# Staging the diagonal blocks of the gated delta rule with ScalarE copies instead of a masked product and a strided sum

## The chip, the cores and the metric

The kernel runs on one core of a Trainium2 chip. The core has five engines, each with its own instruction stream that it works off in order: TensorE (PE; its weight loads are shown as PEld), VectorE (DVE), ScalarE (ACT), GpSimd (POOL) and SyncE (SP), which here only issues DMA transfers. The metric is the device time of one execution in microseconds (us); of several executions the median is given.

## The reference, cut to what matters

The kernel computes a two-layer decoder trunk for one sequence of 512 positions and width 1024. The first layer mixes the sequence with a gated delta rule (8 heads of 128), the second with differential attention; each is followed by an MLP of width 4096. The change lies in the gated delta rule:

```python
kb = kc * bc[..., None]
a_mat = jnp.where(strict, jnp.einsum('bhnik,bhnjk->bhnij', kb, kc) * decay, 0.0)
rhs = jnp.concatenate([vc * bc[..., None], kb * jnp.exp(gcum)[..., None]], axis=-1)
sol = lax.linalg.triangular_solve(eye + a_mat, rhs, left_side=True, lower=True, unit_diagonal=True)
```

For every head and every chunk of the sequence a unit lower triangular matrix (identity plus `a_mat`) has to be inverted, or a system with it solved. The reference uses chunks of 64 positions; the kernel uses four chunks of 128, which gives the same result, and works with the transposed matrix.

## The kernel before, in words

The kernel goes through its stages in the order of the reference: norm and modulation, the projections of the first layer with the gated delta rule inside them, the output projection, the first MLP, attention, the second MLP. Weights come in with SyncE's DMAs (`weights`, L288 to L297): ScalarE rounds a block to a high part (L293), VectorE or GpSimd takes the low part (L284), and PE multiplies three times (`three`, L299 to L302). Beside that, VectorE works off 112 dot products for the conditioning vector, a few at each weight block (`mod_dot`, L193).

The function `gdn(h)` (from L509) does one head of the delta rule and is a generator with three parts. Its first part builds the matrices and inverts them, the second runs over the four chunks in sequence, the third normalises the output. The loop at L730 projects head after head and starts each head's first two parts, then finishes the head before.

Within the first part the steps that matter here are these.

1. L549 to L559: for each of the four chunks PE forms two 128x128 products in a PSUM bank "a" (tag "pa"; there are two such banks), and VectorE scales them into the SBUF tile "bq" (L558). A half of "bq" holds two chunks, each as the matrix B (128 columns) followed by the matrix ATT (128 columns). B is the transposed triangular matrix; `B(n)` and `ATT(n)` pick them for chunk n.
2. L568 to L574: the eight 16x16 blocks on each B's diagonal are taken out. VectorE multiplies B by a mask that is one in these blocks (`m_sub`, tile "db"), and sums over the eight block columns, so that row p keeps 16 values, those of its own block (tile "dc": 128 partitions x 4 chunks x 16).
3. L575 to L578: "dc" is written to a tile "d1" in DRAM and read back as "mt", with one 16x16 block on each of 32 partitions (4 chunks x 8 blocks). Both are DMAs of SyncE's queue; the read waits until the write has landed.
4. L579 to L587: 15 steps of a triangular solve on "mt", two VectorE instructions each (L584, L586), invert the 32 blocks.
5. L588 to L595: the inverses go through DRAM once more ("d2", back as "tc") and are spread to the diagonals of 128x128 tiles "t" (L593).
6. L596 to L639: PE, VectorE and ScalarE join blocks of 16 to blocks of 32, 64 and 128 ("t", "z", "um", "pi"), with copies on ScalarE at L624.
7. L641 to L654: this head's v and q are transposed by PE (L513, banks "pa") and read out by ScalarE (L649 and L520).

The second part (from L657) uses "z" and "ATT". All tiles named here but "d1", "d2" (DRAM) and the PSUM banks lie in one SBUF pool, `g_pool`, where tiles of one tag take turns in `bufs` buffers.

Nothing in the source fixes the order in which an engine meets work of different heads. The tile framework plans each engine's order when the program is built, by the order in the source as priority and by its own estimate of when operands are ready; it also places the semaphores. On the chip each engine then follows its fixed order.

Of the kernel before, what the change touches and what calls it, by code (L numbers as in the profile page):

```python
# [10 lines left out]
F32 = mybir.dt.float32  # L11
F32R = mybir.dt.float32r
AF = mybir.ActivationFunctionType
ALU = mybir.AluOpType
AX = mybir.AxisListType
PSUM = bass.MemoryType.PSUM

P = 128
D = 1024
KT = D // P  # L20
S = 512
# [8 lines left out]
SUB = 16  # L30
# [55 lines left out]
def trunk_kernel(ctx: ExitStack, tc: tile.TileContext, a, outT):  # L86
    nc = tc.nc
    V, G, A, T = nc.vector, nc.gpsimd, nc.scalar, nc.tensor
# [3 lines left out]
    def nm(s):  # L92
        count[0] += 1
        return f"{s}_{count[0]}"

    def open_pool(name, side="left", bufs=1):
        st = ExitStack()
        p = st.enter_context(tc.tile_pool(name=nm(name), bufs=bufs, side=side, reuse_waits="tile"))
        return p, st
# [14 lines left out]
    dp = ctx.enter_context(tc.tile_pool(name="dp", bufs=3, space=bass.MemoryType.DRAM))  # L114
# [13 lines left out]
    def big(pool, tag, bufs, dt=F32):  # L128
        return pool.tile([P, S], dt, tag=tag, name=nm(tag), bufs=bufs)
# [10 lines left out]
    def v3(ap, n=P):  # L140
        return ap.rearrange("p (u f) -> p u f", f=n)
# [231 lines left out]
    for k in range(KT):  # L373
        n = NE[k]
# [53 lines left out]
    g_pool, g_st = open_pool("g", "right")  # L428
# [10 lines left out]
    def gt_(name):  # L439
        return cp.tile([P, NT, H], F32, name=name)  # L440

    u, e, w, l, g = gt_("g_u"), gt_("g_e"), gt_("g_w"), gt_("g_l"), gt_("g_g")
# [58 lines left out]
    def uu(t, n):  # L501
        return t[:, n * P:(n + 1) * P]

    def m4(ap):
        return ap.unsqueeze(1).to_broadcast([P, 4, P])

    m_sub = mask[:, M_L1:M_L1 + P]

    def gdn(h):  # L509
# [36 lines left out]
        V.tensor_tensor(out=sj, in0=sj, in1=beta[:, :, h], op=ALU.mult)  # L546


        bq = [big(g_pool, "bq", 6) for _ in range(2)]  # L549
        for n in range(2):  # L550
            ps = bank("a")
            for c in (2 * n, 2 * n + 1):
# [3 lines left out]
            for c in (2 * n, 2 * n + 1):  # L556
                o = (c % 2) * 256
                V.scalar_tensor_tensor(out=v3(bq[n][:, o:o + 256]), in0=v3(ps[:, o:o + 256]), scalar=sj[:, c:c + 1],  # L558
                                       in1=uu(ex, c).unsqueeze(1).to_broadcast([P, 2, P]), op0=ALU.mult, op1=ALU.mult)  # L559
# [5 lines left out]
            return bq[n // 2][:, (n % 2) * 256 + P:(n % 2) * 256 + 256]  # L565


        db = big(g_pool, "db", 1)  # L568
        for n in range(2):
            V.tensor_tensor(out=v3(db[:, n * 256:(n + 1) * 256]),  # L570
                            in0=bq[n].rearrange("p (u t f) -> p u t f", u=2, t=2)[:, :, 0, :],
                            in1=m_sub.unsqueeze(1).to_broadcast([P, 2, P]), op=ALU.mult)
        dc = g_pool.tile([P, 4, SUB], F32, tag="dc", name=nm("dc"), bufs=2)
        V.tensor_reduce(out=dc, in_=db.rearrange("p (u b c) -> p u c b", u=4, c=SUB), axis=AX.X, op=ALU.add)  # L574
        d1 = dp.tile([4, P, SUB], F32, tag="d1", name=nm("d1"))  # L575
        nc.sync.dma_start(d1.rearrange("u p c -> p u c"), dc)
        mt = g_pool.tile([32, SUB, SUB], F32, tag="mt", name=nm("mt"), bufs=2)
        nc.sync.dma_start(mt.rearrange("p r c -> p (r c)"), d1.rearrange("u (b r) c -> (u b) (r c)", r=SUB))  # L578
        xv = g_pool.tile([32, SUB, SUB], F32, tag="xv", name=nm("xv"), bufs=2)  # L579
        pr = g_pool.tile([32, SUB, SUB], F32, tag="pr", name=nm("pr"), bufs=2)  # L580
        G.tensor_copy(xv, eye)
        for s in range(SUB - 1):
            shp = [32, SUB - 1 - s, s + 1]
            V.tensor_tensor(out=pr[:, s + 1:, :s + 1], in0=mt[:, s, s + 1:].unsqueeze(2).to_broadcast(shp),  # L584
                            in1=xv[:, s, :s + 1].unsqueeze(1).to_broadcast(shp), op=ALU.mult)
            V.tensor_tensor(out=xv[:, s + 1:, :s + 1], in0=xv[:, s + 1:, :s + 1], in1=pr[:, s + 1:, :s + 1],  # L586
                            op=ALU.subtract)  # L587
# [6 lines left out]
                        in0=tc_.unsqueeze(2).to_broadcast([P, 4, P // SUB, SUB]),  # L594
                        in1=m4(m_sub).rearrange("p u (b c) -> p u b c", c=SUB), op=ALU.mult)  # L595
# [20 lines left out]
        for b in (32, 64):  # L616
# [13 lines left out]
            if b == 32:  # L630
                p0, p1 = parts[0]
                for n in range(4):
# [3 lines left out]
                                in1=v3(pz[p1, 0:4 * b], b), op=ALU.subtract)  # L636
            for p0, p1 in parts:
                V.tensor_tensor(out=v3(z)[p0, :, p1], in0=v3(z)[p0, :, p1], in1=v3(pz[p0, 0:4 * b], b),
                                op=ALU.subtract)  # L639
# [28 lines left out]
        for c in range(NT):  # L668
            r = uu(vn, 0)
            if c > 0:  # L670
# [5 lines left out]
                r = g_pool.tile([P, P], F32, tag="r", name=nm("r"), bufs=2)  # L676
# [53 lines left out]
    for h in range(H):  # L730
        proj_head(h)
        heads.append(gdn(h))
        next(heads[h])
        next(heads[h])
        if h:
            next(heads[h - 1], None)
# [275 lines left out]
```

## Time and profile before

| what | us |
|---|---|
| median of 3 runs | 1369.26 |
| lowest and highest of them | 1368.76, 1371.17 |
| profiled execution | 1367.7 |
| its span, first to last instruction | 1365.9 |
| PE busy | 1304.3 |
| DVE busy | 829.7 |
| ACT busy | 558.8 |
| POOL busy | 471.1 |

Busy times are of the profiled execution and are unions: two overlapping instructions of one engine count once. Consecutive matmuls overlap, so that PE can be busy without a gap and still not be at its highest rate. In rows of groups the columns are line, engine, operation, tiles written and read, shapes and count, then total busy time, mean duration of one in ns, and the engine's idle time just before them with what ended it. In rows of a timeline the first two numbers are start and duration in us, counted from the start of the span. In rows of waits the columns are total, number and longest.

### The profile page before, as it was taken

Reading aid. Unit: us, or ns where it says so; the run is one execution under the profiler, and the core shown is the slowest. Engines: PE = TensorE matmul, PEld = TensorE weight load, DVE = VectorE, ACT = ScalarE, POOL = GpSimd, SP = SyncE. Lnnn points to the kernel's source line nnn. Section 1 sums busy time; section 2 is a strip of 40 time slices with the busy share of each in tenths; the row PEclk is TensorE's granted clock in tenths of the full one; section 3 lists DMA queues with packets and bytes.
Section 4 is the critical chain, followed back from the end, with each engine's and each line's share of the span. In section 5 each row is a group of like instructions: output and inputs, shape, how many; then the busy total and the mean of one; then the engine's idle time right before and its main releaser. Section 6 shows DMA issues by size and latency. Waiting matters only on the chain. (4 is left out here: it accounts for less than half of the span.)

```text
span 1365.9 us, 19395 instructions
## 1 busy us (share of the span) xinstructions
PE 1304.3 (95%) x7240; PEld 1097.0 (80%) x7240; DVE 829.7 (61%) x1632; ACT 558.8 (41%) x1175; POOL 471.1 (34%) x281
## 2 busy tenths in 40 slices
PE   4888999999999999999999999999999999999997
PEld 4666878777799888888888978888898888888886
DVE  6979899787847887778851777777453200031113
ACT  3396556553535342234422453444344421143221
POOL 4324132220015444444443021232144444444441
PEclk9999999899999999999999999999999999999998
DMA  9633323125624767766642232222123322232221
GB/s 316 213 93 96 107 71 93 37 75 141 209 103 146 252 222 243 242 229 228 221 154 93 66 120 86 66 67 66 62 79 110 105 94 93 100 102 93 93 77 62
DMA packets 113214, 174.98 MB, mean 128 GB/s; under 512 B 16384, under 2 KB 56992, under 8 KB 113120
## 3 DMA queue, kind: packets, MB, share of 16 engines
q1 hardware_dynamic: 112416, 172.92, 39.7%
q8 instruction: 57, 0.93, 0.3%
q10 hardware_dynamic: 704, 0.83, 0.2%
q14 instruction: 37, 0.30, 0.1%
HBM read 170.04 MB, written 2.62 MB: 126 GB/s over the span
## 5 line engine op out<-in xcount | busy, mean ns | idle before, releaser
L284 POOL TENSOR_TENSOR wl<-raw,wh 128x1024 fp32r<-128x1024 f32 (+1 forms) x137 | 330.1, 2410 | 392.1 <-ACT wh L293 392.1
L293 ACT ACTIVATE wh<-raw 128x1024 fp32r<-128x1024 f32 (+2 forms) x217 | 216.2, 997 | 468.6 <-PE pj L301 242.9
L300 PE MATMUL pj<-h,wh 128*128 128x512 f32 (+1 forms) x816 | 291.2, 360 | 12.4 <-ACT h L278 6.7
L302 PE MATMUL pj<-h,wl 128*128 128x512 f32 (+1 forms) x816 | 290.5, 358 | 1.9 <-DVE wl L284 1.9
L301 PE MATMUL pj<-h,wh 128*128 128x512 f32 (+1 forms) x816 | 291.2, 357 | 0.0
L193 DVE SCALAR_TENSOR_TENSOR mw<-mw,one,cs 128x1024 f32<-128x1024 f32 x96 | 209.4, 2194 | 47.5 <-ACT one L213 47.3
L300 PEld LDWEIGHTS pj<-h,wh 128*128 128x128 f32 x816 | 155.7, 191 | 33.3 <-ACT h L278 8.8
L302 PEld LDWEIGHTS pj<-h,wl 128*128 128x128 f32 x816 | 156.2, 192 | 20.1 <-DVE wl L284 2.6
L301 PEld LDWEIGHTS pj<-h,wh 128*128 128x128 f32 x816 | 156.4, 192 | 17.1
L302 PE MATMUL pj<-u,wl 128*128 128x512 f32 (+1 forms) x448 | 160.9, 359 | 0.0
L301 PE MATMUL pj<-u,wh 128*128 128x512 f32 (+1 forms) x448 | 160.9, 359 | 0.0
L300 PE MATMUL pj<-u,wh 128*128 128x512 f32 (+1 forms) x448 | 160.8, 359 | 0.0
L346 DVE SCALAR_TENSOR_TENSOR x<-pj,mod,x 128x256 f32<-128x256 f32 (+1 forms) x53 | 30.2, 585 | 152.2 <-PE pj L302 152.2
L284 DVE TENSOR_TENSOR wl<-raw,wh 128x1024 fp32r<-128x1024 f32 (+2 forms) x80 | 86.4, 1082 | 23.5 <-ACT wh L293 23.3
L300 PEld LDWEIGHTS pj<-u,wh 128*128 128x128 f32 x448 | 84.6, 189 | 12.7 <-issue 0.2
L301 PEld LDWEIGHTS pj<-u,wh 128*128 128x128 f32 x448 | 84.6, 189 | 12.6
L302 PEld LDWEIGHTS pj<-u,wl 128*128 128x128 f32 x448 | 84.6, 189 | 12.5
L768 DVE SCALAR_TENSOR_TENSOR pj<-pj,r 128x512 f32<-128x512 f32 x32 | 21.6, 691 | 51.9 <-ACT r L767 51.7
L300 PE MATMUL pn<-h,wh 128*128 128x512 f32 x128 | 49.8, 389 | 0.0
L301 PE MATMUL pn<-h,wh 128*128 128x512 f32 x128 | 49.8, 389 | 0.0
L302 PE MATMUL pn<-h,wl 128*128 128x512 f32 x128 | 49.8, 389 | 0.0
L300 PE MATMUL pm<-h,wh 128*128 128x512 f32 x128 | 49.8, 389 | 0.0
(298 smaller groups left out, 2386.5 us busy)
## 6 DMA issues: line engine op xcount, KB each, us to landing
raw<-in_mlp_w_dram SPq DMA_DIRECT2D x128, 512.0 KB, 3.6
mw<-in_mod_wT_dram SPq DMA_DIRECT2D x96, 512.0 KB, 4.8
raw<-in_a_w_in_dram SPq DMA_DIRECT2D x96, 128.0 KB, 2.7
mw<-in_kv_mod_wT_dram SPq DMA_DIRECT2D x16, 512.0 KB, 5.3
raw<-in_kv_w_dram SPq DMA_DIRECT2D x16, 512.0 KB, 3.2
x<-in_xT_dram SPq DMA_DIRECT2D x16, 256.0 KB, 5.8
raw<-in_a_w_in_dram SPq DMA_DIRECT2D x16, 256.0 KB, 2.8
raw<-in_a_w_out_dram SPq DMA_DIRECT2D x8, 512.0 KB, 4.1
```

The source lines that it names most:

```text
L193: V.scalar_tensor_tensor(out=w, in0=w, scalar=one, in1=cs, op0=ALU.mult, op1=ALU.mult, accum_out=raw_mod[:, c:c + 1])
L284: (V if n else G).tensor_tensor(out=out, in0=x, in1=hi.bitcast(F32), op=ALU.subtract)
L293: A.activation(wh, raw, AF.Copy)
L300: T.matmul(ps, lhsT=wh, rhs=xh, start=first, stop=False, skip_group_check=skip)
L301: T.matmul(ps, lhsT=wh, rhs=xl, start=False, stop=False, skip_group_check=skip)
L302: T.matmul(ps, lhsT=wl, rhs=xh, start=False, stop=last, skip_group_check=skip)
L346: V.scalar_tensor_tensor(out=x[d][:, sl], in0=ps[j][:, sl], scalar=mod[:, gt + d:gt + d + 1], in1=x[d][:, sl], op0=ALU.mult, op1=ALU.add)
L768: V.scalar_tensor_tensor(out=ps[j], in0=ps[j], scalar=0.0, in1=r, op0=ALU.max, op1=ALU.mult)
```

## The change: what it does

The two halves of "bq" become one tile with two halves, and the pool keeps three of these instead of six halves. The mask, the product and the sum (step 2) go, with the tile "db". In their place ScalarE copies, for each of the four groups of 32 partitions, the 32 columns of B that lie on the diagonal beside it, for all four chunks in one instruction: "dc" grows to 128 x 4 x 32 and holds the 32x32 diagonal blocks. The DRAM tile "d1" grows likewise. The read back picks the 16x16 blocks: one DMA for the even blocks (rows 0 to 15 and columns 0 to 15 of each 32x32 block) and one for the odd ones (rows and columns 16 to 31), each to 16 of the 32 partitions of "mt". What stands in "mt", and all that follows, is unchanged.

```diff
-        bq = [big(g_pool, "bq", 6) for _ in range(2)]
+        bqt = g_pool.tile([P, 2, S], F32, tag="bq", name=nm("bq"), bufs=3)
+        bq = [bqt[:, n] for n in range(2)]
...
-        db = big(g_pool, "db", 1)
-        for n in range(2):
-            V.tensor_tensor(out=v3(db[:, n * 256:(n + 1) * 256]),
-                            in0=bq[n].rearrange("p (u t f) -> p u t f", u=2, t=2)[:, :, 0, :],
-                            in1=m_sub.unsqueeze(1).to_broadcast([P, 2, P]), op=ALU.mult)
-        dc = g_pool.tile([P, 4, SUB], F32, tag="dc", name=nm("dc"), bufs=2)
-        V.tensor_reduce(out=dc, in_=db.rearrange("p (u b c) -> p u c b", u=4, c=SUB), axis=AX.X, op=ALU.add)
-        d1 = dp.tile([4, P, SUB], F32, tag="d1", name=nm("d1"))
+        dc = g_pool.tile([P, 4, 32], F32, tag="dc", name=nm("dc"), bufs=2)
+        for g in range(0, P, 32):
+            A.activation(dc[g:g + 32], bqt.rearrange("p n (u t f) -> p (n u) t f", u=2, t=2)[g:g + 32, :, 0, g:g + 32],
+                         AF.Copy)
+        d1 = dp.tile([4, P, 32], F32, tag="d1", name=nm("d1"))
         nc.sync.dma_start(d1.rearrange("u p c -> p u c"), dc)
         mt = g_pool.tile([32, SUB, SUB], F32, tag="mt", name=nm("mt"), bufs=2)
-        nc.sync.dma_start(mt.rearrange("p r c -> p (r c)"), d1.rearrange("u (b r) c -> (u b) (r c)", r=SUB))
+        for e in range(2):
+            nc.sync.dma_start(mt[e::2], d1.rearrange("u (g e r) c -> (u g) e r c", e=2, r=SUB)[:, e, :, e * SUB:(e + 1) * SUB])
```

## The prediction

> **What bounds the kernel now.** I read the page first: how long is each engine busy?
>
> ```profile
> span 1365.9 us, 19395 instructions
> PE 1304.3 (95%) x7240; PEld 1097.0 (80%) x7240; DVE 829.7 (61%) x1632; ACT 558.8 (41%) x1175; POOL 471.1 (34%) x281
> ```
>
> TensorE (PE) sets the whole. That average says nothing of the stage in which the edited lines run, so I asked for the busy times by stretch; the columns are the stretch, its length, then busy time and count of PE, weight loads, VectorE (DVE), ScalarE (ACT) and GpSimd (POOL), the granted TensorE clock, the DMA share and GB/s.
>
> ```profile
> 93.00:229.00 136.00, 125.92 (x881) 101.36 (x880) 124.17 (x382) 87.42 (x259) 47.91 (x37) 0.99 0.32 87
> 229.00:365.00 136.00, 131.12 (x878) 105.39 (x877) 109.80 (x308) 68.31 (x191) 24.51 (x21) 0.96 0.37 103
> 365.00:700.00 335.00, 332.36 (x1655) 282.54 (x1655) 258.96 (x302) 124.79 (x232) 138.92 (x59) 1.00 0.64 212
> ```
>
> The edited lines run eight times, once a head, between 93 and 365 us. In the first half of that stage DVE is busy 124.17 of 136 us (91%) and PE 125.92 (93%): both are nearly full. In the second half DVE has 81% and PE 96%. In the 335 us behind that PE is busy 99%, so what PE gains in the stage is not swallowed by a later wait but reaches the end of the kernel.
>
> PE is idle 10.08 + 4.88 = 14.96 us in the stage. Which engine ends those gaps? The view of waits from 93 to 365 us, in order of total time (us, times, longest):
>
> ```profile
> PE pj L300 <- DVE cv L483: 2.3, 3, 1.6
> PE pa L513 <- DVE bq L558: 2.2, 2, 1.5
> PE pa L513 <- DVE pr L584: 2.0, 1, 2.0
> PE pj L302 <- DVE wl L284: 1.6, 1, 1.6
> PE pi L622 <- DVE t L614: 1.6, 1, 1.6
> PE pi L598 <- DVE t L593: 1.2, 1, 1.2
> PE pr L679 <- DVE r L677: 1.2, 3, 0.5
> PE pr L671 <- DVE st L691: 0.8, 2, 0.5
> PE pr L684 <- DVE y L682: 0.8, 2, 0.4
> ```
>
> These nine longest all end on DVE; they add up to 13.7 us. So in this stage PE waits for DVE, at many places and nowhere long; ACT is in none of the nine. That is the case for an edit that takes work from DVE and gives it to ACT.
>
> **What the change removes.** Two masked products (L570) and one strided reduction (L574) a head, on DVE:
>
> ```profile
> L574 DVE TENSOR_REDUCE dc<-db 128x64 f32<-128x512 f32 x8 | 8.2, 1025 | 0.0
> L570 DVE TENSOR_TENSOR db<-bq,mask 128x256 f32<-128x256 f32 x16 | 6.3, 410 | 0.0
> ```
>
> By busy time that is 14.5 us. Instructions of one engine overlap a little, so I count from start to start where they follow each other. DVE around head 0's block (start, duration):
>
> ```profile
> 94.74 1.66 DVE L558 SCALAR_TENSOR_TENSOR bq<-pa,sj,ex 128x256 f32<-128x256 f32 x4
> 96.32 0.75 DVE L570 TENSOR_TENSOR db<-bq,mask 128x256 f32<-128x256 f32 x2
> 96.98 0.16 DVE L644 TENSOR_TENSOR kd<-sj,eg_all 128x4 f32<-128x4 f32 x1
> ...
> 98.26 1.03 DVE L574 TENSOR_REDUCE dc<-db 128x64 f32<-128x512 f32 x1
> 99.21 0.74 DVE L483 SCALAR_TENSOR_TENSOR cv<-pj,cols,cv 128x511 f32<-128x511 f32 x1
> ```
>
> The two products take 96.98 - 96.32 = 0.66 us and the reduction 99.21 - 98.26 = 0.95, together 1.61 us a head, 12.9 us for eight. How much of it reaches PE has bounds of 0 (DVE only idles longer) and 12.9 (DVE alone sets the stage; the 13.7 us of PE's waits would just hold it). Six of the eight reductions lie before 229 us, the last of these at 228.44. There I take one half, since PE and DVE are equally full and each holds up the other: 6 x 1.61 x 0.5 = 4.8 us. For the two heads behind, where DVE has 19% idle, one quarter: 2 x 1.61 x 0.25 = 0.8. Sum: 5.6 us gained.
>
> **What it adds on ACT.** Four copies a head of 32 partitions x 128 elements. ACT does such copies already, from PSUM:
>
> ```profile
> L624 ACT ACTIVATE um<-pi 32x128 f32<-32x128 f32 x16 | 4.3, 270 | 11.6 <-PE pi L622 11.3
> L649 ACT ACTIVATE vn<-pa,nk 128x128 f32<-128x128 f32 x32 | 9.6, 372 | 9.1 <-PE pa L513 9.1
> ```
>
> Four by 0.27 us are 1.08 us a head, 8.6 us in all, on an engine busy 87.42 + 68.31 = 155.7 of 272 us (57%). Its idle time hides them. Without that cover they cost up to 8.6 us: behind them on ACT stand this head's L649 and L520 (source order), which empty the two "pa" PSUM banks, and PE's transposes (L513) wait for those. The bounds are 0 and 8.6; I take 0.9 us, a tenth, near the lower end, since no row of PE's waits above is ended by ACT.
>
> **The path through DRAM.** The staging write waits for ACT in place of the reduction; the read back becomes two DMAs. SyncE's queue at heads 0 and 1, and the DMA table (KB each, median us to landing):
>
> ```profile
> 99.32 0.37 SPq L576 DMA_DIRECT2D d<-dc  x1
> 102.53 0.34 SPq L578 DMA_DIRECT2D mt<-d  x1
> 105.99 1.41 SPq L291 DMA_DIRECT2D raw<-in_a_w_in_dram  x3
> 109.83 0.37 SPq L576 DMA_DIRECT2D d<-dc  x1
> ```
>
> ```profile
> out_dram<-x SPq DMA_DIRECT2D x16, 128.0 KB, 1.8
> d<-dc SPq DMA_DIRECT2D x8, 32.0 KB, 1.8
> mt<-d SPq DMA_DIRECT2D x8, 32.0 KB, 1.9
> tc<-d SPq DMA_DIRECT2D x8, 32.0 KB, 2.1
> ```
>
> The write grows from 32 to 64 KB (512 pieces of 128 bytes instead of 64); as many pieces, and a 128 KB write lands in the same 1.8 us, so I add nothing. The read of 32 rows of 1 KB becomes 512 pieces of 64 bytes. "tc" (L591) reads just such pieces today: 2.1 us against 1.9, hence +0.2. The second read is issued 0.34 us after the first, so the tile "mt" is complete 0.5 us later than one read would make it. Against that, head 0's write was issued 2.9 us after its last bq (94.74 + 1.66 = 96.40 to 99.32), and with four copies at once it could follow after 1.1. So "mt" may land from 1.3 us earlier to 0.5 later, and more if ACT is held up. I take 0: DVE's first solve step is seldom waiting for it, as the idle time before L584 shows.
>
> ```profile
> L584 DVE TENSOR_TENSOR pr<-mt,xv 32x15 f32<-32x15 f32 (+7 forms) x120 | 26.7, 230 | 0.7
> ```
>
> On SyncE itself the extra issue is 8 x 0.34 = 2.7 us (bounds 0 and 2.7). Queued behind both reads are the weight loads (L291), and behind those ACT's split of the weights (L293). SyncE was free for 3.1 us between the read's issue (102.87) and the next weight load (105.99), so I take 0.
>
> [...]
>
> **The rest of the edit.** Six half tiles "bq" become three whole ones: the same memory, three heads deep as before, cost 0. "db" goes and later tiles of the pool move in SBUF; no row shows a price of an address, so 0. One thing has no row at all: the order on each engine is not source order. Head 1's bq stands among head 0's solve steps:
>
> ```profile
> 106.31 0.17 DVE L586 TENSOR_TENSOR xv<-xv,pr 32x15 f32<-32x15 f32 x1
> 106.41 0.47 DVE L558 SCALAR_TENSOR_TENSOR bq<-pa,sj,ex 128x256 f32<-128x256 f32 x1
> ```
>
> The tile framework plans it when the program is built, from its own costs, so removed and added instructions shift the neighbours of everything in the stage. Taken as 0, with a third of PE's 14.96 us of idle time, 5 us either way, for the range.
>
> **The sum.** -5.6 + 0.9 = -4.7 us. The profiled execution took 1367.7 us (span 1365.9, 1.8 around it), so 1363.0; the runs' median, 1369.26, lies 1.56 above it, so 1364.6 as a median. What a measurement of this kernel can tell from no change is 0.2%, 2.7 us: 1366.5 to 1372.0.
>
> **The rivals.**
>
> *DVE only idles longer.* PE is 93 to 96% busy in the stage, and DVE's own waits may grow by what it saves. For it: many short waits on as many different DVE lines rather than one late line. Against it: every long wait of PE ends on DVE. Gain 0 to 2.7, time 1369.
>
> *ACT becomes the late one (slower).* The plan puts the copies where ACT stands waiting for PE; the write, both reads and the first L584 then come late, and DVE, in order, stops there with weights (L284) and convolutions (L483) queued behind. What speaks for it, ACT's longest waits in the stage:
>
> ```profile
> ACT wh L293 <- PE pj L301: 24.3, 22, 2.7
> ACT um L624 <- PE pi L622: 21.3, 11, 4.5
> ```
>
> It decides once the delay exceeds the lead of "mt" over its use, which is small at some heads: at head 5 the read is issued at 232.37, lands 1.9 later, and is used at 234.55, 0.3 us of lead.
>
> ```profile
> 232.37 0.41 SPq L578 DMA_DIRECT2D mt<-d  x1
> ...
> 234.55 0.17 DVE L584 TENSOR_TENSOR pr<-mt,xv 32x15 f32<-32x15 f32 x1
> ```
>
> Price: the copies' full 8.6 us, and of the 12.9 only a quarter (3.2) gained: +5.4, 1374.7. Against it: ACT has 116 us idle in the stage, and the copies need only bq.
>
> *The half-clock stretch goes.* Once in the stage TensorE ran at half clock for 10 us, soon after PE had stood 1.57 us waiting for L614:
>
> ```profile
> 244.72 0.59 PE L622 MATMUL pi<-t,bq 32*32 32x32 f32 x16 [1.57 <-DVE t L614]
> ...
> 246.20:256.30 10.10, 10.10 (x56) 7.62 (x52) 4.60 (x12) 5.01 (x7) 1.77 (x2) 0.50 0.00 1
> ```
>
> PE was busy all of it, so half, 5.05 us, was lost. If a lighter DVE removes that stall, this comes on top: 1364.6 - 5.05 = 1359.5. Against it: gaps as long remain, and a new one could cost as much elsewhere. [...]
>
> *All of it arrives.* DVE alone sets the stage, and the copies are free: 1369.26 - 12.9 = 1356.4.
>
> **How the numbers follow.** Forecast 1364.6: 0.37. DVE idles: 0.22. ACT late: 0.22. Clock: 0.13. All arrives: 0.06. Faster is 0.37 + 0.13 + 0.06 = 0.56, same 0.22, slower 0.22. The range runs from 1355 (all arrives, a little below) to 1374 (nearly the slower rival, and 5 us of planning on top of "idles"); the likeliest case alone, 5 us of planning about it, has 1359.6 to 1369.6.
>
> **What would show it.** L570 and L574 are gone and DVE's busy time in the stage falls from 234 us by about 14; four ACT groups of 32x128 at about 0.27 us each appear; two issues a head land in about 2 us. The forecast is right if PE's idle time in the stage falls by about 5 us with DVE still its main releaser. "Idles": DVE's idle time grows by 13 and PE's stays at 15. "ACT late": idle time before L584 rises above its 0.7 us, ended by the DMA, or PE's L513 waits for ACT. "Clock": the row at 0.50 is missing. I am wrong altogether if the time moves while DVE's and PE's sums in the stage do not, or if the difference arises behind 365 us.

## The result, and the profile after

The kernel after takes 1362.28 us (median of 5 executions, 1360.07 to 1362.44) against 1369.02 us before (5 executions). The ratio is 0.9948, with a 95% interval of 0.9936 to 0.9960: 6.7 us or 0.5% faster. Forecast were 1364.6 us, 4.7 below the median before. The profiled execution took 1360.07 us. Three executions in a slow state (1615, 6459 and 1837 us), all among the experiments further below, are left out of every median.

The page of the kernel after, its first lines:

```profile
span 1358.2 us, 19398 instructions
...
PE 1298.0 (96%) x7240; PEld 1093.0 (80%) x7240; DVE 816.5 (60%) x1608; ACT 566.4 (42%) x1207; POOL 465.9 (34%) x281
```

DVE is busy 13.2 us less than before (829.7), ACT 7.6 more (558.8). The span is 7.7 us shorter. Where is that won? The same stretches as before (length, busy time and count of PE, weight loads, DVE, ACT, POOL, then the granted clock, DMA share and GB/s):

```profile
93.00:229.00 136.00, 126.70 (x902) 102.73 (x902) 119.62 (x375) 95.94 (x293) 47.35 (x40) 1.00 0.36 92
229.00:365.00 136.00, 129.84 (x894) 105.09 (x893) 108.62 (x305) 71.75 (x198) 21.98 (x20) 1.00 0.41 116
```

Two things are to be seen. PE is idle as long as before: 272 - 256.54 = 15.46 us against 14.96. And the granted clock is 1.00 in both halves, where it was 0.99 and 0.96. Time at half clock counts as busy (from 106.20 to 109.60 us before, PE is busy 3.40 of 3.40 us at a clock of 0.50), so a gain by the clock does not show in the idle time.

These windows do not hold the same work before and after. A mark that the same work stands ahead of is the first MLP's first matmul into a bank "pn" (L300): it starts at 437.6 us before and at 429.8 after, 7.8 us earlier, so the whole difference arises ahead of it. From 93 us to that matmul, before and then after:

```profile
93.00:437.60 344.60, 326.99 (x2252) 272.20 (x2252) 278.75 (x770) 184.34 (x503) 92.68 (x69) 0.98 0.35 103
```

```profile
93.00:429.80 336.80, 319.60 (x2255) 267.51 (x2255) 266.01 (x746) 192.80 (x537) 87.21 (x69) 1.00 0.38 106
```

PE has the same matmuls to within three. Its idle time is 17.6 us before and 17.2 after; its busy time falls by 7.4. Before, PE was at half clock in this stretch for 13.65 us (3.41 and 10.24, shown below), which costs half of that, 6.8 us, if PE sets the pace there (an estimate: 128x512 matmuls that follow each other start 0.43 us apart at half clock, at 106.42 and 106.85 us before, and 0.23 apart at full clock, at 105.11 and 105.34 after); after, never. So in these two profiles nearly all of the gain is clock, and 0.4 us of it is shorter waiting. The work taken from DVE is seen as well: 278.75 - 266.01 = 12.74 us.

PE's waits after, the longest of the stage (total, times, longest):

```profile
PE pr L513 <- POOL o L702: 2.3, 1, 2.3
PE pa L513 <- DVE bq L559: 2.1, 2, 1.4
PE pa L532 <- ACT vn L648: 1.7, 2, 1.2
PE pj L302 <- DVE wl L284: 1.7, 1, 1.7
PE pi L621 <- DVE t L613: 1.5, 3, 0.9
PE pi L609 <- DVE um L606: 1.4, 1, 1.4
PE pr L678 <- DVE r L676: 1.1, 4, 0.3
```

DVE is still the main releaser. New are the first row, a wait for GpSimd, and the third: PE waits for ACT's "vn", which stands behind the four copies on ACT.

At one place a gap before can be followed to DVE. Before, PE twice stood for 1.6 us within five microseconds, for a convolution (L483) and for the low part of a weight block (L284), both queued on DVE behind head 0's masked product and sum. PE's timeline of the kernel before:

```profile
102.94 0.50 PE L300 MATMUL pj<-h,wh 128*128 128x512 f32 x1 [1.57 <-DVE cv L483]
...
105.98 0.65 PE L302 MATMUL pj<-h,wl 128*128 128x512 f32 x1 [1.58 <-DVE wl L284]
```

DVE's timeline before, and then after, at that weight block:

```profile
104.97 0.95 DVE L284 TENSOR_TENSOR wl<-raw,wh 128x768 fp32r<-128x768 f32 x1
```

```profile
102.86 0.94 DVE L284 TENSOR_TENSOR wl<-raw,wh 128x768 fp32r<-128x768 f32 x1
```

The block is ready 2.1 us earlier, and after the change PE runs through this place:

```profile
103.37 0.40 PE L301 MATMUL pj<-h,wh 128*128 128x512 f32 x1
103.85 0.50 PE L302 MATMUL pj<-h,wl 128*128 128x512 f32 x1
104.18 0.40 PE L300 MATMUL pj<-h,wh 128*128 128x512 f32 x1
```

The two gaps before had a sequel, as had the gap at 244.72 that the prediction showed. Stretches of 3.41 us of the kernel before, ahead of a half-clock stretch and in it:

```profile
102.79:106.20 3.41, 1.68 (x5) 0.82 (x6) 2.94 (x10) 3.40 (x5) 1.01 (x1) 1.00 0.04 10
106.20:109.60 3.40, 3.40 (x11) 2.71 (x11) 3.40 (x13) 0.67 (x4) 0.00 (x0) 0.50 0.47 116
242.71:246.12 3.41, 1.84 (x29) 1.00 (x30) 3.28 (x8) 0.54 (x2) 0.14 (x1) 1.00 0.00 0
246.12:249.53 3.41, 3.41 (x35) 2.48 (x32) 2.49 (x7) 0.69 (x1) 0.00 (x0) 0.50 0.00 0
```

Each time PE was busy about half of the stretch, and the clock was halved in the next. In the kernel after neither half-clock stretch is there. That the gaps bring the half clock on is argued from this order in time; the last section has stretches that were filled as little and that full clock followed.

### The profile page after: what moved, and what is told of

The parts are those of the page before. It is cut to its first block, busy times and chain, and to the rows that moved or that the text cites. A ratio compares the mean times of both kernels' runs of the same rounds, so it can differ in the third digit from the quotient of the medians.

```text
span 1358.2 us, 19398 instructions
## 1 busy us (share of the span) xinstructions
PE 1298.0 (96%) x7240; PEld 1093.0 (80%) x7240; DVE 816.5 (60%) x1608; ACT 566.4 (42%) x1207; POOL 465.9 (34%) x281
## 5 line engine op out<-in xcount | busy, mean ns | idle before, releaser
L284 POOL TENSOR_TENSOR wl<-raw,wh 128x1024 fp32r<-128x1024 f32 (+1 forms) x137 | 329.3, 2404 | 393.0 <-ACT wh L293 389.1
L300 PE MATMUL pj<-h,wh 128*128 128x512 f32 (+1 forms) x816 | 289.5, 358 | 9.8 <-ACT h L278 5.4
L300 PEld LDWEIGHTS pj<-h,wh 128*128 128x128 f32 x816 | 155.1, 191 | 30.4 <-ACT h L278 7.2
L300 PE MATMUL pj<-u,wh 128*128 128x512 f32 (+1 forms) x448 | 160.8, 359 | 0.0
L284 DVE TENSOR_TENSOR wl<-raw,wh 128x1024 fp32r<-128x1024 f32 (+2 forms) x80 | 84.2, 1054 | 25.8 <-ACT wh L293 25.4
L300 PEld LDWEIGHTS pj<-u,wh 128*128 128x128 f32 x448 | 84.6, 189 | 12.8 <-issue 0.2
L300 PE MATMUL pn<-h,wh 128*128 128x512 f32 x128 | 49.8, 389 | 0.0
L300 PE MATMUL pm<-h,wh 128*128 128x512 f32 x128 | 49.8, 389 | 0.0
```

The source lines that it names most:

```text
L284: (V if n else G).tensor_tensor(out=out, in0=x, in1=hi.bitcast(F32), op=ALU.subtract)
L300: T.matmul(ps, lhsT=wh, rhs=xh, start=first, stop=False, skip_group_check=skip)
```

## The experiments

Two theories were to be told apart. **DVE load**: the 12.9 us taken from DVE reach PE in part. **Plan or clock**: any edit makes the framework lay out the stage anew, and with the gaps the half-clock stretches fall elsewhere; 6.7 us would then be luck of one plan. Each time is a median, each ratio is to the kernel before on the same chip, with its 95% interval.

### The kernel before, profiled again

No edit.

> The kernel before, unchanged, profiled once more, to see whether the half-clock stretch of 10 us at 246 us belongs to the program or to one execution. If it belongs to the program (a fixed order of work with a fixed stall), the new profile has it again near 246 us and the time stays within 0.2% of 1369. If it belongs to an execution, the new profile lacks it or has it elsewhere, and executions of this one program differ by about 5 us with their clock.

Measured: 1368.36 us, ratio 0.9995 (0.9985 to 1.0004). In the new profile the granted clock of the stage's two halves is 0.99 and 0.96, as in the first profile, which had its half-clock stretches at 106.17 us (3.41 long) and 246.12 (10.24 long). So the half-clock time of the stage comes with the program, as far as two profiles can show it. Executions still differ: among 31 of the kernel before that ran beside the second group of experiments, time and mean clock go together (1362.98 us at 0.992, 1371.93 at 0.986; correlation -0.90). A line fitted within each of 16 such sets of executions (one program on one chip each) and pooled gives -0.89 us per 0.001 of mean clock. Half-clock time in which PE has little to do is in the mean clock too: the last 7.04 us of the kernel before's span and the last 5.91 of the kernel after's are at 0.50, with PE busy for 0.48 and 0.00 us of them. Such time should cost little, so the line is no upper bound for what the clock costs.

### The merged "bq" alone

```diff
-        bq = [big(g_pool, "bq", 6) for _ in range(2)]
+        bqt = g_pool.tile([P, 2, S], F32, tag="bq", name=nm("bq"), bufs=3)
+        bq = [bqt[:, n] for n in range(2)]
```

> The kernel before with only the first part of the change: the two halves of bq become one tile, three buffers instead of six halves. Theory DVE load: nothing is taken from DVE, so 1369, within 2.7 us. Theory plan: the framework plans the stage anew even for this, so the time moves by some us without any work being removed; then part of the 6.7 us of the change may be that.

Measured: 1365.07 us, ratio 0.9977 (0.9962 to 0.9992), 3.0 us below the kernel before. Every engine has its instructions in the same order as before, so neither theory explains the 3 us: nothing is removed and no order planned anew. Two readings are left. Either differences of 2 to 3 us between single kernels carry no meaning by themselves, even with an interval that excludes zero, or the merge is itself worth up to 3 of the 6.7 us. It is in every kernel after, so the pairs further below do not part the two, and no run under a second plan has the merge alone.

### The removed work put back

After, with the old lines beside the new ones; the sum goes into a tile that nobody reads, so the output is the reference's.

```diff
+        db = big(g_pool, "db", 1)
+        for n in range(2):
+            V.tensor_tensor(out=v3(db[:, n * 256:(n + 1) * 256]), ...)
+        dx = g_pool.tile([P, 4, SUB], F32, tag="dx", name=nm("dx"), bufs=1)
+        V.tensor_reduce(out=dx, in_=db.rearrange("p (u b c) -> p u c b", u=4, c=SUB), axis=AX.X, op=ALU.add)
         dc = g_pool.tile([P, 4, 32], F32, tag="dc", name=nm("dc"), bufs=2)
```

> The kernel after with the removed DVE work put back beside it: the two masked products and the strided sum of each head run again, into a tile that nobody reads; ScalarE's copies and the DMAs stay as in after. Theory DVE load: the gain is given back and about 1 us more, so 1367 to 1370. Theory plan or clock: the time has no fixed tie to DVE's load and stays near 1362, or goes anywhere within 5 us.

Measured: 1367.95 us, ratio 0.9995 (0.9982 to 1.0009): 5.7 us above after (6.4 by the ratios, as the two were timed in different groups). The gain is gone, as the theory DVE load has it, but not into waits: PE is busy 1305.5 us in its profile against 1298.0 after, and idle 60.7 against 60.2. Two stretches at the start of the stage:

```profile
104.39:107.80 3.41, 1.58 (x6) 0.60 (x5) 3.03 (x12) 3.38 (x10) 1.36 (x2) 1.00 0.00 0
107.80:118.04 10.24, 8.04 (x24) 6.24 (x25) 10.17 (x27) 10.15 (x37) 6.14 (x4) 0.50 0.27 58
```

A half-clock stretch is back, behind a stretch with PE busy 1.58 of 3.41 us while DVE is busy 3.03. Load and clock therefore need not exclude each other: a loaded DVE can make the gap, and half clock can follow the gap. Not all of the 5.7 us can be laid to the work put back, though: in this profile the granted clock is 0.99 from 365 to 700 us too, against 1.00 after, where that work does not run.

### The removed work put back twice

As above, with the products and the sum run twice a head.

> The kernel after with the removed products and sums run twice a head on DVE, unread: twice the dose of the run that put them back once, which came out 5.7 us above after's median. Theory DVE load: about as much again or more, since DVE then is nearly full in the whole stage, so 1373 to 1382. Theory plan or clock (no tie to the load): 1362 to 1370, as the single dose.

Measured: 1365.71 us, ratio 0.9979 (0.9966 to 0.9992). The expectation of the theory DVE load, 1373 to 1382, is missed by at least 7 us, and twice the work is no slower than once the work. DVE is busier, as meant: in this kernel's stage from 93 to 365 us the rows of the added work are

```profile
L576 DVE TENSOR_REDUCE dx<-db 128x64 f32<-128x512 f32 x16 | 16.4, 1024 | 0.0
...
L571 DVE TENSOR_TENSOR db<-bq,mask 128x256 f32<-128x256 f32 x32 | 12.8, 407 | 0.0
```

So time does not follow DVE's load in proportion. A share of several us for the plan would explain it; this run does not show it.

### The ScalarE copies as an addition

The kernel with merged "bq" and the old product and sum, and the four copies besides, into a tile that nobody reads.

```diff
         V.tensor_reduce(out=dc, ...)
+        dy = g_pool.tile([P, 4, 32], F32, tag="dy", name=nm("dy"), bufs=1)
+        for g in range(0, P, 32):
+            A.activation(dy[g:g + 32], bqt.rearrange(...)[g:g + 32, :, 0, g:g + 32], AF.Copy)
```

> The kernel with the merged bq and the old masked product and sum, and beside them the four ScalarE copies of each head into a tile that nobody reads. Theory that the copies are hidden on ScalarE: within 1 us of the run with the merged bq alone (0.9 us was the prediction's price). Theory that they delay the readout of the pa banks behind them: 3 to 8.6 us slower than that run.

Measured: 1368.95 us, ratio 1.0009 (0.9999 to 1.0019). That is 3.9 us above the kernel with the merged "bq" (4.4 by the ratios), and 1.2 us above the kernel before by the ratio (0.0009 x 1369). Since these two have the same instruction order, both are fair references, and the copies, with the new plan that they bring, cost 1 to 4 us. They are not quite hidden; where it shows in this kernel, from 93 to 365 us (the row has 0.4 us in the kernel with the merged "bq"):

```profile
PE pa L532 <- ACT vn L654: 2.9, 2, 1.7
```

This kernel and the one with the removed work put back have the same work on DVE and ACT; they differ in which tile feeds the path through DRAM, and in its DMAs. Their times, 1368.95 and 1367.95, give no sign that the new DMAs cost anything.

### The copies on VectorE

```diff
-            A.activation(dc[g:g + 32], bqt.rearrange(...)[g:g + 32, :, 0, g:g + 32], AF.Copy)
+            V.tensor_copy(dc[g:g + 32], bqt.rearrange(...)[g:g + 32, :, 0, g:g + 32])
```

> The kernel after with its four 32x128 copies a head on DVE instead of ScalarE (tensor_copy); no mask, no sum. Copies of 128x128 take DVE 0.28 us, so about 4 x 0.2 = 0.8 us a head stay on DVE, half of the old 1.61. Theory DVE load: half of the gain is lost, 1365 to 1366. Theory that ScalarE's copies cost something of their own: no slower than after, or a little faster, 1361 to 1363.

Measured: 1369.62 us, ratio 1.0004 (0.9992 to 1.0015): neither expectation. The first rested on 0.2 us a copy; they take 0.35:

```profile
L571 DVE COPY dc<-bq 32x128 f32<-32x128 f32 x32 | 11.1, 346 | 0.6
```

That puts 11.1 us on DVE in place of 14.5, so three quarters of the load stay. In proportion the theory DVE load would then have some 1367.5 us; the measured time is 2 us above.

### No copies at all

Four DMAs a head write the diagonal blocks from "bq" to DRAM.

```diff
-        dc = g_pool.tile([P, 4, 32], F32, tag="dc", name=nm("dc"), bufs=2)
-        for g in range(0, P, 32):
-            A.activation(dc[g:g + 32], ..., AF.Copy)
-        nc.sync.dma_start(d1.rearrange("u p c -> p u c"), dc)
+        bv = bqt.rearrange("p n (u t f) -> p (n u) t f", u=2, t=2)
+        for g in range(0, P, 32):
+            nc.sync.dma_start(d1[:, g:g + 32].rearrange("u p c -> p u c"), bv[g:g + 32, :, 0, g:g + 32])
```

> The kernel after without any copy: four DMAs a head write the 32x32 diagonal blocks to the DRAM tile straight from bq, the read back is as in after. Takes 1.2 us a head off ScalarE and adds three DMA issues to SyncE. Theory that ScalarE's copies are hidden: within 1.5 us of after, 1361 to 1364. Theory that they hold up the pa banks or the staging write: 2 to 6 us faster than after, 1356 to 1360.

Measured: 1369.40 us, ratio 1.0002 (0.9985 to 1.0019): neither expectation. ACT has the least to do of all kernels here (555.5 us), DVE about as little as in the kernel after (820.8 us against 816.5 and 819.8 in its two profiles), and nothing is gained. Its profile has a long half-clock stretch in mid-stage:

```profile
216.39:219.80 3.41, 2.59 (x49) 2.15 (x49) 2.72 (x7) 3.13 (x15) 0.16 (x1) 1.00 0.00 0
219.80:230.04 10.24, 10.24 (x43) 8.14 (x41) 4.74 (x20) 2.67 (x6) 0.85 (x1) 0.50 0.16 40
```

By this run taking work from DVE is not enough; whether the plan or the three further DMA issues a head are to blame, it does not say.

### The kernel after, again

No edit.

> The kernel after, unchanged, beside the other runs of this group. Its ratio to before should be 0.995 again (1361 to 1363). What its new profile tells: if the missing half-clock stretch near 246 us made the gain, a profile without it goes with the low time once more; with such a stretch of 10 us it should be some 5 us slower.

Measured: 1361.50 us, ratio 0.9951 (0.9934 to 0.9968). The result holds, and the second profile again has no half-clock stretch between 93 and 365 us.

### The change under two other plans

If 6.7 us were luck of one plan, the difference between before and after should come out otherwise once both are planned anew. Two moves within `gdn` that add and remove nothing were made in both kernels. The first writes two small products earlier:

```diff
         V.tensor_tensor(out=sj, in0=sj, in1=beta[:, :, h], op=ALU.mult)
+        nk = col(4, "nk")
+        V.tensor_tensor(out=nk, in0=ssk, in1=rk, op=ALU.mult)
+        kd = col(4, "kd")
+        V.tensor_tensor(out=kd, in0=sj, in1=kde[:, :, h], op=ALU.mult)
...
-        nk = col(4, "nk")
-        V.tensor_tensor(out=nk, in0=ssk, in1=rk, op=ALU.mult)
-        kd = col(4, "kd")
-        V.tensor_tensor(out=kd, in0=sj, in1=kde[:, :, h], op=ALU.mult)
```

> The kernel before, with the same instructions, but two small VectorE products of gdn (nk and kd, 128x4 each) written some 95 lines earlier, right behind sj; the plan of the stage comes out otherwise. Theory plan: the time moves by 2 to 6 us either way without any work being added or removed, with the clock moving along. Theory DVE load: within 2.7 us of 1369.

> The kernel after with the same move of nk and kd. Theory DVE load: 5 to 7 us faster than the kernel before with that move. Theory plan: the difference between these two has no reason to be 6.7 us again; anything from -8 to +6, and this kernel itself is slower than 1362 with more chance than faster, since 1362 is the lowest of the plans tried.

The second writes the block of q ahead of that of v:

```diff
+        ssq = sumsq(natural(qT[h]), "sqq")
+        V.tensor_scalar(out=ssq, in0=ssq, scalar1=float(P), scalar2=EPS * P, op0=ALU.mult, op1=ALU.add)
+        rq = col(4, "rq")
+        G.tensor_tensor(out=rq, in0=ssq, in1=mhalf[:, 0:4], op=ALU.pow)
         pv = natural(vT[h])
...
-        ssq = sumsq(natural(qT[h]), "sqq")
-        V.tensor_scalar(out=ssq, in0=ssq, scalar1=float(P), scalar2=EPS * P, op0=ALU.mult, op1=ALU.add)
-        rq = col(4, "rq")
-        G.tensor_tensor(out=rq, in0=ssq, in1=mhalf[:, 0:4], op=ALU.pow)
```

> The kernel before, with the same instructions, but the block that transposes and squares q (ssq, rq) written ahead of the one that transposes v. Theory plan: 2 to 6 us either way, with the clock. Theory DVE load: within 2.7 us of 1369.

> The kernel after with the same exchange of the q and v blocks. Theory DVE load: 5 to 7 us faster than the kernel before with that exchange. Theory plan: a difference of any size from -8 to +6. Over the three pairs (this one, the one with nk and kd moved, and the change itself) the mean difference says what the change is worth apart from the plan: 0 to 3 us by the theory plan, 5 to 7 by the theory DVE load.

Measured, with the mean clock of each kernel's executions:

| plan | before's lines | after's lines | difference, by the ratios | clock before, after |
|---|---|---|---|---|
| as given (second group) | 1369.25 | 1361.50, 0.9951 (0.9934 to 0.9968) | -7.8, -6.7 | 0.9889, 0.9944 |
| nk and kd early | 1373.59, 1.0040 (1.0027 to 1.0053) | 1367.13, 0.9993 (0.9981 to 1.0004) | -6.5, -6.4 | 0.9887, 0.9936 |
| q ahead of v | 1369.19, 1.0007 (0.9993 to 1.0021) | 1362.79, 0.9963 (0.9952 to 0.9973) | -6.4, -6.0 | 0.9910, 0.9935 |

The plan alone moves the time by up to 5.1 us (1373.59 against 1368.52, the kernel before in that group). Yet the change is worth 6.0 to 7.8 us in all three, which is what the theory DVE load expected and the theory of a lucky plan did not. And in all three the clock is higher after the change.

How the gain reaches PE is read from the profiles of the four pairs, one execution each. All of them have the same 7240 matmuls, so PE's busy time is the same work:

| pair of profiles, before and after | span | PE busy | PE idle |
|---|---|---|---|
| as given, first | 1365.9, 1358.2 | 1304.3, 1298.0 | 61.6, 60.2 |
| as given, again | 1364.4, 1358.9 | 1303.5, 1297.9 | 60.9, 61.0 |
| nk and kd early | 1368.2, 1363.3 | 1302.3, 1299.4 | 65.9, 63.9 |
| q ahead of v | 1364.0, 1362.5 | 1302.8, 1301.4 | 61.2, 61.1 |

In every pair most of what the span lost is busy time, 6.3, 5.6, 2.9 and 1.4 us: the same matmuls took less. The idle time changed by -1.4, +0.1, -2.0 and -0.1 us. The last pair's profiles lie only 1.5 us apart, against 6.4 us between the medians, so they say little of that pair.

## How far the prediction was right, point by point

**What bounds the stage.** Right in part: PE waits for DVE in it, before and after, and with the removed work put back the gain was gone. That shorter waits would be the gain was not so.

**The gain of 5.6 us from DVE.** The direction held, the mechanism for the most part did not. The prediction let PE's waits shrink by one half or one quarter of what DVE saves; PE's idle time, net of all costs, shrank by 0 to 2 us in the four pairs. The rest of the gain came as less busy time for the same matmuls; in the first two pairs, whose stage loses all of its half-clock time (13.65 us in the first), that is full clock in place of half. The prediction had this as a rival with a chance of 0.13, to come on top of the forecast; it came in place of most of it. Of the half-clock stretches in the stage the prediction counted one (5.05 us); there are two, at 106.17 and 246.12, with 13.65 us and so up to 6.8 to lose. That the forecast lies within 2.3 us of the measured time is luck in so far as the two sizes are alike.

**The price of 0.9 us on ACT.** Too low, with the place named rightly. A copy takes 304 ns, not 270, and PE waits for "vn" behind the copies at the "pa" banks, 1.7 us in the profile after. The group of the kernel after from 93 to 365 us:

```profile
L571 ACT ACTIVATE dc<-bq 32x128 f32<-32x128 f32 x32 | 9.7, 304 | 0.6 <-DVE bq L559 0.4
```

With the copies at 1 to 4 us, DVE's relief and the clock together must have brought more than the net 6.0 to 7.8.

**The path through DRAM at 0.** The single prices were low: each read lands in 2.4 us instead of 2.1, and one issue takes 0.60 us of SyncE instead of 0.34. The write of 64 KB lands in 2.4 us in the profile of the kernel after, where 1.8 was taken; in the two kernels with the work put back and the one with copies on VectorE it does land in 1.8. The DMA table after, the issue's row, and the first solve step:

```profile
d<-dc SPq DMA_DIRECT2D x8, 64.0 KB, 2.4
mt<-d SPq DMA_DIRECT2D x16, 16.0 KB, 2.4
```

```profile
L577 SPq DMA_DIRECT2D mt<-d x16: 567/596/684, 102.2 to 299.3; - x16
```

```profile
L583 DVE TENSOR_TENSOR pr<-mt,xv 32x15 f32<-32x15 f32 (+7 forms) x120 | 24.5, 209 | 1.3
```

DVE's idle time before the solve steps rose from 0.7 to 1.3 us, so the path stayed hidden, as taken.

**The plan at 0, with 5 us either way.** The bound was about right: the two moves that changed nothing but the plan gave +5.1 and +0.7 us.

**The rivals.** "DVE only idles longer" describes the waits well: PE's idle time stayed. "The half-clock stretch goes" came true as an event: both stretches of the stage are gone in both profiles of the kernel after. The prediction priced the two apart; together they give 1369.26 - 6.8 = 1362.5, nearest to the measured 1362.28. "ACT becomes the late one" fell with the result, though its mechanism is real in small.

**What should have shown it.** L570 and L574 are gone and the four copies are there. DVE's busy time between 93 and 365 us fell by only 5.7 us (233.97 to 228.24), because that window holds more work after; over the same work it fell by 12.7. The sign that the forecast was to be known by, PE's idle time in the stage falling by about 5 us, did not come; over the same work it fell by 0.4. The sign of the clock, no row at 0.50, did come. The sign of being wrong altogether, a difference that arises behind 365 us, did not: the last matmul that reads "bq" (L685, L684 after) starts at 355.3 us instead of 365.4.

**What stays open.** Why the half-clock stretches go. A lighter DVE that leaves fewer gaps close together fits the three pairs and the work put back, but it is argued: the kernel without copies has as light a DVE and half-clock time at two places (granted clock 0.96 from 93 to 127 us and 0.95 from 127 to 229), and twice the work put back costs no more than once. With a plan's share of up to 5 us in every single kernel, only pairs under several plans would tell, and these two have none. Open too is whether the merged "bq" has a part in the gain.

## What to carry to other kernels

Where a framework plans the order of instructions, one kernel against another measures the edit and a new plan together, here up to 5 us each; make a small move that changes only the plan in both kernels and compare pairs. Read the granted clock by stretch before reading PE's idle time: half-clock time looks like work (here PE was busy for all of 10.24 us at 0.50). And compare PE's busy time for the same matmuls: here it fell while the waits stayed, so the gain was not the one that the waits had promised.

## What the runs showed of the hardware

In the kernel before, the half-clock stretches of the stage last 3.41 us (from 106.17) and 10.24 us (from 246.12). PE was not idle throughout the 3.41 us ahead of them: it was busy for 1.68 and 1.84 us. In the kernel with the removed work put back, 10.24 us at half clock (from 107.80) came behind 1.58 us busy of 3.41, and in the kernel without copies 10.24 us (from 219.80) behind 2.59. Full clock followed stretches filled as little: in the kernel after, PE was busy 1.74 us from 116.66 to 120.07 and 1.60 us from 362.42 to 365.83, and the clock in the 3.41 us behind each was 1.00. So PE's busy time just ahead does not tell the two cases apart here; what does was not shown. Nor did a busy PE end a stretch at once: from 246.12 us in the kernel before and from 219.80 in the kernel without copies PE was busy for all of 10.24 us at half clock.

The same 32x128 copy of 4-byte elements from SBUF takes 304 ns on ScalarE (kernel after) and 346 ns on VectorE (the kernel with the copies there).
